# Splitting the attention's projection weights ahead of time, during the first MLP, with the parts kept in DRAM

## The chip, the cores and the metric

The kernel runs on one core of a Trainium2 chip. The metric is the device time of one execution in microseconds, as a median over runs. The engines are TensorE (PE, with its weight loads as PEld), VectorE (DVE), ScalarE (ACT), GpSimd (POOL) and SyncE (SP), which here only issues transfers.

## The reference

A decoder trunk of two layers over 528 positions (16 learned meta tokens and 512 inputs) of width 1024, all in float32. Layer 0 mixes with an mLSTM head group and a gated linear recurrence, layer 1 with differential attention; each is followed by an MLP with a squared ReLU:

```python
for layer in range(DEPTH):
    hn = _rmsnorm(h, norm_mix[layer])
    h = h + (_ab_mixer(hn, ...) if layer % 2 == 0 else _diff_attn(hn, c_w_in, ..., c_w_out, ...))
    h = h + _sq_relu_mlp(_rmsnorm(h, norm_mlp[layer]), mlp_w1[layer], mlp_w2[layer])
h = _rmsnorm(h, norm_final)

def _diff_attn(hn, w_in, ...):
    q, k, v = _split(hn @ w_in, C_SPLITS)      # 8 heads; q and k rotated on 16 of 64 dims
    ...                                        # two softmaxes per head, subtracted; norm per head
    return o @ w_out
```

## The kernel before

All large products run in float32r, at three products for one: each float32 operand is split into a high part (a cast to float32r) and a low part (the rest, a subtraction), and high x high, high x low and low x high are added up in PSUM.

**Weight units.** All projection weights lie in DRAM as 225 units `wu[u]` of 128 x 1024 floats (512 KB). Their order of use is the list `seq`: units 0 to 48 for layer 0's input projections, 49 to 64 for its output projection, 65 to 128 for the first MLP (`U_MLP0`), 129 to 152 for the attention's q, k and v (`U_QKV`, three per head), 153 to 160 for its output projection (`U_OUT1`), 161 to 224 for the second MLP (`U_MLP1`). `get_w` hands out the next unit and first calls `emit_load` until two units beyond it are on their way. `emit_load` (L148) transfers the unit into a buffer `raw` (two buffers, pool `wr`), casts it on ACT into `wh` (L159) and subtracts on DVE, or on POOL for the positions listed in `POOL_L`, into `wl` (`sub`, L115). `wh` and `wl` have three buffers each (pool `wp`), so ACT's cast of a unit waits until PE is done with the unit three places earlier. The cast and the subtraction stand under `soon()`, a raised priority. `unit_mm` (L177) multiplies a unit with eight blocks of the activations.

**MLP.** `mlp` (L651) works in four quarters: eight units of the first matrix, each followed by a squared ReLU (DVE L662, ACT L664) and the split of the result, and eight units of the second matrix, each added to the residual `h` (DVE L673).

**Attention.** `attend` (L730) runs the three units of a head. The q and k results are copied out (ACT L741), rotated with a shuffle (L747), two products (POOL L748, DVE L749) and a sum (L750), split (L754, L758) and moved into the layouts for the score products by transfers `st<-rh` and `st<-rl` (SP, L765 and L766). Between and inside the units stand the steps of earlier heads, placed by hand in `SLOTS`: `sstep` (scores L805 to L809, row maximum L811 to L816, exponential L819), `tstep` (transposes L841, their split L853), `vstep` (transposes of v, L787), `ostep` (L865) and `fstep` (norm, L875 to L881). The output projection (L903) interleaves with the last heads.

**Order.** The Tile framework orders the instructions of every engine at compile time, by priority and a model of the durations, and inserts the waits; each engine's queue then runs in that order. PSUM has four buffers for the units and four for the rest.

Of the kernel before, what the change touches and what calls it, by code (L numbers as in the profile page):

```python
# [10 lines left out]
F32 = mybir.dt.float32  # L11
F32R = mybir.dt.float32r
# [4 lines left out]
P = 128  # L17
# [20 lines left out]
U_MLP0 = 65  # L38
# [14 lines left out]

POOL_OPS = "Mm"

POOL_L = {5, 33, 43, 44, 52, 126, 140, 143, 149, 151, 155, 159, 161, 164}
N_S = 31

N_KZ = 3
LOAD1 = 9  # L60
# [4 lines left out]
C_NMIX0, C_NMIX1, C_NMLP0, C_NMLP1, C_NFIN, C_MN, C_CW, C_CB, C_BR, C_BI, C_LAM, C_SUB, C_IB, C_FB = (  # L65
    0, 8, 16, 24, 32, 40, 48, 80, 88, 96, 104, 112, 113, 114)
# [3 lines left out]
def unit_of(t):  # L70
    a = [int(c) for c in t[1:]]
    if t[0] == "q":
        return U_HEAD + 6 * a[0] + a[1]
    if t[0] == "e":
        return U_GATE
    if t[0] == "o":
        return U_O + a[0]
    return U_LRU + 4 * (a[0] // 2) + a[0] % 2 + (2 if t[0] == "g" else 0)


def trunk(tc, hT, wu, wri, pk, lv, rope, gf, out, probe=None):
    nc = tc.nc
    ctx = ExitStack()

    def dump(name, ap):
        if probe and name in probe:
            nc.sync.dma_start(out=probe[name], in_=ap)

    with ctx:
        cp = ctx.enter_context(tc.tile_pool(name="cp", bufs=1))  # L90
        wr = ctx.enter_context(tc.tile_pool(name="wr", bufs=2))
        wp = ctx.enter_context(tc.tile_pool(name="wp", bufs=3))
# [3 lines left out]
        dr = ctx.enter_context(tc.tile_pool(name="dr", bufs=1, space=bass.MemoryType.DRAM))  # L96
# [7 lines left out]
        def sc(name, dt=F32, w=T):  # L104

            return big.tile([P, T], dt, tag="s", name=name, bufs=N_S)

        def xt(name):

            hi = big.tile([P, T], F32R, tag="x", name=name + "h", bufs=32)  # L110
            lo = big.tile([P, T], F32R, tag="x", name=name + "l", bufs=32)
            return hi, lo

        def sub(eng, o, a, b):
            eng.tensor_tensor(out=o, in0=a, in1=b, op=ALU.subtract)  # L115

        def split(hl, src, sl=slice(0, T), eng=None):
            nc.scalar.copy(hl[0][:, sl], src)
            sub(eng or nc.vector, hl[1][:, sl], src, hl[0][:, sl].bitcast(F32))
# [15 lines left out]
        def soon():  # L135
            return tc.high_priority(offset=BOOST)
# [4 lines left out]

        seq = list(range(N_UNIT))
        ready = []
        seq[0:U_OUT0] = [unit_of(t) for t in PLAN if t[0] in "qeocg"]
        seq[U_OUT0:U_OUT0 + 16] = [U_OUT0 + (8 + i) % 16 for i in range(16)]
        state = {"next": 0, "use": 0}

        def emit_load():  # L148
            i = state["next"]
            u = seq[i]  # L150
            raw = wr.tile([P, 1024], F32, tag="raw", name=f"raw{i}")
            nc.sync.dma_start(out=raw, in_=wu[u])
            if u >= N_UNIT - 8:
                wh, wl = (wp.tile([P, 1024], F32R, tag="wf" + p, name=f"w{p}{i}", bufs=8) for p in "hl")
            else:
                wh = wp.tile([P, 1024], F32R, tag="wh", name=f"wh{i}")
                wl = None if u == U_GATE else wp.tile([P, 1024], F32R, tag="wl", name=f"wl{i}")
            with soon():
                nc.scalar.copy(wh, raw)  # L159
                eng = nc.gpsimd if i in POOL_L else nc.vector  # L160
                if u == U_GATE:

                    hi, r = (a.rearrange("p (k c) -> p k c", k=KB) for a in (wh, raw))
                    sub(eng, hi[:, :, 64:100], r[:, :, 0:36], hi[:, :, 0:36].bitcast(F32))
                else:
                    sub(eng, wl, raw, wh.bitcast(F32))
            ready.append((wh, wl))
            state["next"] += 1

        def get_w(u):  # L170
            while state["next"] <= min(state["use"] + 2, len(seq) - 1):
                emit_load()
            assert seq[state["use"]] == u
            state["use"] += 1
            return ready.pop(0)

        def unit_mm(u, x, lo=0, n=T, mid=None):  # L177

            wh, wl = get_w(u)
            mid = mid or state.pop("mid", None)  # L180
            cuts = [(lo, n)] if n <= 512 else [(0, HV), (HV, HV)]
            ps = [mmt(f"mm{u}") for _ in cuts]
            for k in range(KB):
                if k == KB // 2 and mid:
                    mid()
                c = slice(k * P, (k + 1) * P)
                terms = [(wh, x[k][0]), (wh, x[k][1])] + ([(wl, x[k][0])] if wl is not None else [])
                for j, (w, xx) in enumerate(terms):
                    for p, (s, m) in zip(ps, cuts):
                        nc.tensor.matmul(p[:, :m], w[:, c], xx[:, s:s + m], start=(k == 0 and j == 0),  # L190
                                         stop=(k == KB - 1 and j == len(terms) - 1))
            return [(p[:, :m], slice(s, s + m)) for p, (s, m) in zip(ps, cuts)]
# [33 lines left out]
        def norm_x(h, gc, lo, tag, late=False):  # L226

            x = [xt(f"{tag}x{k}") for k in range(KB)]
            fin = []
            for k in range(KB):  # L230
                hk = h[:, k, lo:]
                fin_x = nc.scalar.activation(out=x[k][0][:, lo:], in_=hk, func=AF.Copy, scale=pc(gc + k))  # L232
                nc.vector.scalar_tensor_tensor(out=x[k][1][:, lo:], in0=hk, scalar=pc(gc + k),
                                               in1=x[k][0][:, lo:].bitcast(F32), op0=ALU.mult, op1=ALU.subtract)
                if not late:
                    norm_sq(h, lo, k, fin)
            return (x, fin_x) if late else (x, fin)
# [9 lines left out]
        def norm_r(terms, lo, tag, le=False):  # L247

            w = (T - lo) // 2
            ps = [axt("nps") for _ in range(2)]  # L250
            for b in range(2):
                nc.tensor.matmul(ps[b][:, :w], ones, terms[0][:, lo + b * w:lo + (b + 1) * w], start=True, stop=True)
            v = sc("nv")
            for b in range(2):
                idn = nc.scalar.activation(out=v[:, lo + b * w:lo + (b + 1) * w], in_=ps[b][:, :w], func=AF.Identity,
                                     bias=epsc, scale=1.0 / 1024)
            rstd = big.tile([P, T], F32, tag="rstd", name=tag + "rstd", bufs=2)
            rsq_of(rstd[:, lo:], v[:, lo:], lambda nm: sc(nm)[:, lo:], le=le, after=idn)
            return rstd, v
# [16 lines left out]

        h0 = big.tile([P, KB, T], F32, tag="h", name="h0")
        emit_load()
        for k in range(KB):
            nc.sync.dma_start(out=h0[:, k, :], in_=hT[:, k, :])  # L280
            if k == LOAD1:
                emit_load()
# [365 lines left out]
        dump("h1", h)  # L648


        def mlp(u0, gc, lo, tag, last=None):  # L651
            n = T - lo
            mx, terms = norm_x(h, gc, lo, tag)
            for q in range(4):
                a = []
                for j in range(KB):
                    ps = unit_mm(u0 + q * 16 + j, mx, lo, n)
                    if q == j == 0:
                        rs, _ = norm_r(terms, lo, tag)
                    t = sc("rt")  # L660
                    for p, tk in ps:
                        nc.vector.scalar_tensor_tensor(out=t[:, tk], in0=p, scalar=0.0, in1=rs[:, tk],  # L662
                                                       op0=ALU.max, op1=ALU.mult)
                    nc.scalar.activation(out=t[:, lo:], in_=t[:, lo:], func=AF.Square)  # L664
                    a.append(xt(f"a{j}"))
                    split(a[j], t[:, lo:], slice(lo, T))
                if q == 3 and last:
                    last(a)
                else:
                    for c in range(KB):  # L670
                        ps = unit_mm(u0 + q * 16 + 8 + c, a, lo, n)
                        for p, tk in ps:
                            nc.vector.tensor_tensor(out=h[:, c, tk], in0=p, in1=h[:, c, tk], op=ALU.add)  # L673

        mlp(U_MLP0, C_NMLP0, 0, "m")
        dump("h2", h)


# [212 lines left out]
        for part, ks in enumerate(OUT_K):  # L891
            w = None
            for i, (c, k) in enumerate((c, k) for c in range(KB) for k in ks):
                if i % 8 == 0:
                    w = get_w(U_OUT1 + (6 if part else 0) + i // 8)
# [29 lines left out]
        def final_quarter(a):  # L925
            w = [get_w(N_UNIT - 8 + k) for k in range(KB)]
            for t in range(4):
# [23 lines left out]
                with soon():  # L951
                    if len(spans) == 3:
# [10 lines left out]
                                                   op1=ALU.mult)  # L963
                    nc.sync.dma_start(out=out[t * P:(t + 1) * P, 512:1024], in_=z2)
        mlp(U_MLP1, C_NMLP1, NM, "n", last=final_quarter)


# [93 lines left out]
```

## Time and profile before

| | |
|---|---|
| Median of three runs | 1483.99 us (1482.4 to 1485.17) |
| The profiled execution's own time | 1483.99 us |
| Its span, first to last instruction | 1481.9 us |
| Mean granted clock of TensorE | 0.996 |
| Transfers | 140.79 MB, mean 95 GB/s |
| Casts of weight units on ACT (L159) | 225, 1050 ns each |
| Subtractions of weight units on DVE, on POOL | 210, 1277 ns each; 14, 2418 ns each |

How to read it: a line such as "906.47 0.52 PE L841 MATMUL pt<-ident,e 128\*72 128x128 f32 x3 [1.51 <-DVE vr L774]" says that at 906.47 us from the start PE ran three such matmuls of line 841, which took 0.52 us together, and that it had been idle for 1.51 us, until DVE's instruction of line 774 ended. In a table by stretch the columns are: the stretch, its length, the busy time of each engine with its number of instructions, the granted clock of TensorE (1 is full speed), the mean share of time in which the 16 DMA engines were busy, and GB/s.

### The profile page before, as it was taken

What the parts mean: (1) busy time and instruction counts of PE and PEld (TensorE: products, weight loads), DVE (VectorE), ACT (ScalarE), POOL (GpSimd) and SP (SyncE); (2) the same over time, 40 slices, a digit from 0 to 9 for tenths busy, and PEclk for the clock granted to TensorE, in tenths of its full rate; (3) what the DMA queues carried; (4) which work ended last, traced back from release to release, by engine and by line L of the source; (5) the groups of instructions that cost most, each with busy time, mean ns of one, the idle gap of its engine ahead of it and who ended that gap; (6) DMA issues with size and microseconds to landing.
All of it is one profiled execution on the core that took longest, in us unless ns stands there. A gap on an engine that the chain in (4) does not pass through costs nothing.

```text
span 1481.9 us, 24188 instructions
## 1 busy us (share of the span) xinstructions
PE 1445.6 (98%) x9970; PEld 1344.5 (91%) x9970; DVE 837.7 (57%) x1489; ACT 631.9 (43%) x1090; POOL 126.7 (9%) x100
## 2 busy tenths in 40 slices
PE   8999999999999999999999999999999999999998
PEld 8999999999999999999999988888787888888886
DVE  5867745667545434344344589999865434343452
ACT  6455744647234213233143445655654223132342
POOL 4000001000011000000002211111132000000001
PEclk9999999999999999999999999999999999999999
DMA  7332323231222322322323343323122233233241
GB/s 254 96 114 79 99 72 121 72 100 48 90 93 86 92 95 86 100 86 87 100 86 92 110 115 94 94 87 100 58 86 79 92 100 94 92 100 95 91 124 47
DMA packets 48794, 140.79 MB, mean 95 GB/s; under 512 B 9226, under 2 KB 10775, under 8 KB 48684
## 3 DMA queue, kind: packets, MB, share of 16 engines
q1 hardware_dynamic: 48108, 138.21, 30.4%
q8 instruction: 78, 1.28, 0.4%
q10 hardware_dynamic: 576, 1.05, 0.2%
q14 instruction: 32, 0.26, 0.1%
HBM read 128.55 MB, written 2.16 MB: 88 GB/s over the span
## 4 chain that ended last, share of the span: by engine, by line
PE 85%; DVE 8%; ACT 3%; issue 2%; DMA 1%; POOL 0%; SPq 0%; DVEq 0%; ACTq 0%
PE mm L190 73%; PE mf L940 3%; PE mo L903 3%; PE pnum L393 1%; PE pss L375 1%; PE pg L586 1%; DVE wl L115 1%; DVE qr L750 1%; DMA st<-rh 1%; DVE kz L115 1%; PE pt L841 1%; DVE mx L814 1%; PE po L865 1%; PE psc L805 1%; DVE qs L747 1%
## 5 line engine op out<-in xcount | busy, mean ns | idle before, releaser
L159 ACT CAST wh<-raw 128x1024 fp32r<-128x1024 f32 x225 | 236.3, 1050 | 615.8 <-PE mm L190 510.1
L115 DVE TENSOR_TENSOR wl<-raw,wh 128x1024 fp32r<-128x1024 f32 x210 | 268.1, 1277 | 74.1 <-ACT wh L159 72.0
L673 DVE TENSOR_TENSOR h<-mm,h 128x264 f32<-128x264 f32 (+1 forms) x88 | 41.3, 500 | 188.6 <-PE mm L190 188.6
L243 POOL TENSOR_TENSOR nsq<-nsq 128x528 f32<-128x528 f32 (+1 forms) x28 | 48.4, 1729 | 447.6 <-DVE wl L115 336.0
L662 DVE SCALAR_TENSOR_TENSOR rt<-mm,mrstd 128x264 f32<-128x264 f32 x64 | 24.7, 428 | 89.1 <-PE mm L190 89.1
L662 DVE SCALAR_TENSOR_TENSOR rt<-mm,nrstd 128x512 f32<-128x512 f32 x32 | 22.1, 692 | 79.7 <-PE mm L190 79.6
L115 POOL TENSOR_TENSOR wl<-raw,wh 128x1024 fp32r<-128x1024 f32 x14 | 33.9, 2418 | 230.3 <-ACT wh L159 148.2
L819 ACT ACTIVATE e<-psc,nb 128x264 f32<-128x264 f32 (+3 forms) x80 | 38.1, 481 | 21.3 <-DVE nb L816 18.5
L664 ACT ACTIVATE rt<-rt 128x528 f32<-128x528 f32 (+1 forms) x64 | 40.6, 636 | 2.8 <-DVE rt L662 2.8
L748 POOL TENSOR_TENSOR qr<-qr,tb 128x512 f32<-128x512 f32 (+1 forms) x16 | 26.5, 1654 | 144.9 <-DVE nb L816 82.1
L811 DVE TENSOR_REDUCE mx<-psc 128x1 f32<-128x264 f32 (+3 forms) x80 | 33.2, 429 | 5.8 <-PE psc L809 5.7
L949 POOL TENSOR_TENSOR zg<-z,gfr 128x512 f32<-128x512 f32 x4 | 5.2, 1296 | 343.6 <-issue 326.9
L633 DVE TENSOR_TENSOR h<-mm,h 128x264 f32<-128x264 f32 x32 | 12.4, 428 | 38.7 <-PE mm L190 38.7
L805 PE MATMUL psc<-st,st 128*128 128x264 f32 (+3 forms) x80 | 26.6, 333 | 7.2 <-DVE v1l L115 3.6
L805 PEld LDWEIGHTS psc<-st,st 128*128 128x128 f32 x80 | 15.3, 192 | 14.9 <-ACT e L819 5.3
L853 ACT CAST pp<-pt 128x128 fp32r<-128x128 f32 (+2 forms) x64 | 20.8, 343 | 18.5 <-DVE pp L115 14.0
L190 PE MATMUL mm<-ax0h,wh 128*128 128x264 f32 x98 | 22.0, 297 | 6.1 <-ACT ax0h L232 6.1
L115 DVE TENSOR_TENSOR pp<-pt,pp 128x256 fp32r<-128x256 f32 (+2 forms) x64 | 23.7, 378 | 1.3 <-ACT pp L853 1.1
L806 PE MATMUL psc<-kz,st 128*128 128x264 f32 (+3 forms) x80 | 24.0, 300 | 0.0
L841 PE MATMUL pt<-ident,e 128*72 128x128 f32 (+1 forms) x112 | 18.3, 278 | 5.7 <-ACT e L819 4.2
L190 PE MATMUL mm<-a4h,wl 128*128 128x264 f32 (+1 forms) x88 | 22.6, 316 | 0.0
L190 PE MATMUL mm<-a1h,wh 128*128 128x264 f32 (+1 forms) x88 | 22.5, 316 | 0.0
(802 smaller groups left out, 4772.9 us busy)
## 6 DMA issues: line engine op xcount, KB each, us to landing
raw<-wu SPq DMA_DIRECT2D x225, 512.0 KB
h<-hT SPq DMA_DIRECT2D x16, 264.0 KB
st<-rh SPq DMA_DIRECT2D x32, 132.0 KB
st<-rh SPq DMA_DIRECT2D x16, 128.0 KB
st<-rl SPq DMA_DIRECT2D x16, 128.0 KB
cb<-crow SPq DMA_DIRECT2D x4, 264.0 KB
erb<-crow SPq DMA_DIRECT2D x4, 264.0 KB
rawg<-wri SPq DMA_DIRECT2D x4, 256.0 KB
```

The costliest lines, as they stand in the source:

```text
L115: eng.tensor_tensor(out=o, in0=a, in1=b, op=ALU.subtract)
L159: nc.scalar.copy(wh, raw)
L190: nc.tensor.matmul(p[:, :m], w[:, c], xx[:, s:s + m], start=(k == 0 and j == 0), stop=(k == KB - 1 and j == len(terms) - 1))
L243: nc.gpsimd.tensor_tensor(out=fin[0][:, lo:], in0=fin[0][:, lo:], in1=sq[:, lo:], op=ALU.add)
L662: nc.vector.scalar_tensor_tensor(out=t[:, tk], in0=p, scalar=0.0, in1=rs[:, tk], op0=ALU.max, op1=ALU.mult)
L664: nc.scalar.activation(out=t[:, lo:], in_=t[:, lo:], func=AF.Square)
L673: nc.vector.tensor_tensor(out=h[:, c, tk], in0=p, in1=h[:, c, tk], op=ALU.add)
L805: nc.tensor.matmul(d[:, :m], qS[c][:, qs], kS[c][:, s0:s0 + m], start=True, stop=False)
L811: nc.vector.tensor_reduce(out=mx[:, 2 * c + r:2 * c + r + 1], in_=d[:, :m], axis=AX.X, op=ALU.max)
L819: nc.scalar.activation(out=e[:, s0:s0 + m], in_=d[:, :m], func=AF.Exp, bias=nb, scale=0.125, accum_out=ss[:, c + 2 * r:c + 2 * r + 1])
L903: nc.tensor.matmul(ps, w[ww][:, b], co[k][xx][:, NM:], start=(k == ks[0] and j == 0), stop=(k == ks[-1] and j == 2))
L940: nc.tensor.matmul(pss[n][:, :m], a[k][aa][:, tk], w[k][ww][:, f0:f0 + m], start=(k == 0 and i == 0), stop=(k == KB - 1 and i == 2))
```

## The change

For the positions 129 to 160 of `seq` (`AHEAD`: the 24 units of the attention's q, k and v and the eight of its output projection) the split is made during the first MLP. After every second unit of that MLP `make_ahead` is called, 32 times, and once more after it. A call writes the two parts of the unit made by the call before to DRAM (`parts`, two tiles of 512 KB for each unit), then loads the next unit through the same two `raw` buffers, casts it on ACT and subtracts on DVE into the tiles `wah` and `wal` (one buffer each), without raised priority. When such a unit's turn comes, `emit_load` transfers both parts from DRAM straight into `wh` and `wl`; there is no cast and no subtraction then. Six of these positions leave `POOL_L`.

```diff
-POOL_L = {5, 33, 43, 44, 52, 126, 140, 143, 149, 151, 155, 159, 161, 164}
+POOL_L = {5, 33, 43, 44, 52, 126, 161, 164}
+AHEAD = range(129, 161)
...
+        parts = [[dr.tile([P, 1024], F32, name=f"part{i}{p}") for p in "hl"] for i in AHEAD]
...
         def emit_load():
             i = state["next"]
             u = seq[i]
+            if i in AHEAD:
+                wh, wl = (wp.tile([P, 1024], F32R, tag="w" + p, name=f"w{p}{i}") for p in "hl")
+                for w, part in zip((wh, wl), parts[i - AHEAD[0]]):
+                    nc.sync.dma_start(out=w.bitcast(F32), in_=part)
+                ready.append((wh, wl))
+                state["next"] += 1
+                return
             raw = wr.tile([P, 1024], F32, tag="raw", name=f"raw{i}")
...
+        ahead = list(AHEAD)
+        made = []
+
+        def make_ahead():
+
+            while made:
+                i, hl = made.pop(0)
+                for w, part in zip(hl, parts[i - AHEAD[0]]):
+                    nc.sync.dma_start(out=part, in_=w.bitcast(F32))
+            if ahead:
+                i = ahead.pop(0)
+                raw = wr.tile([P, 1024], F32, tag="raw", name=f"rawa{i}")
+                nc.sync.dma_start(out=raw, in_=wu[seq[i]])
+                hl = [wp.tile([P, 1024], F32R, tag="wa" + p, name=f"wa{p}{i}", bufs=1) for p in "hl"]
+                nc.scalar.copy(hl[0], raw)
+                sub(nc.vector, hl[1], raw, hl[0].bitcast(F32))
+                made.append((i, hl))
...
-        def mlp(u0, gc, lo, tag, last=None):
+        def mlp(u0, gc, lo, tag, last=None, between=None):
...
                     split(a[j], t[:, lo:], slice(lo, T))
+                    if between and j % 2:
+                        between()
...
                             nc.vector.tensor_tensor(out=h[:, c, tk], in0=p, in1=h[:, c, tk], op=ALU.add)
+                        if between and c % 2:
+                            between()
 
-        mlp(U_MLP0, C_NMLP0, 0, "m")
+        mlp(U_MLP0, C_NMLP0, 0, "m", between=make_ahead)
+        make_ahead()
```

## The prediction, made before the changed kernel ran

> **What bounds the kernel now.** I read the page's busy times first, then a table of busy time by stretch (columns: stretch, its length, busy us with instruction counts of PE, PEld, DVE, ACT and POOL, granted clock, DMA share, GB/s).
>
> ```profile
> span 1481.9 us, 24188 instructions
> PE 1445.6 (98%) x9970; PEld 1344.5 (91%) x9970; DVE 837.7 (57%) x1489; ACT 631.9 (43%) x1090; POOL 126.7 (9%) x100
> 460.00:830.00 370.00, 370.00 (x3048) 369.45 (x3047) 156.45 (x233) 116.73 (x148) 13.18 (x7) 1.00 0.30 92
> 835.00:865.00 30.00, 28.16 (x201) 26.28 (x200) 22.48 (x42) 12.36 (x23) 5.27 (x3) 1.00 0.39 106
> 865.00:1068.00 203.00, 187.80 (x1249) 167.74 (x1249) 188.92 (x477) 116.91 (x321) 33.12 (x18) 0.99 0.32 92
> ```
>
> TensorE bounds the whole, but the stages differ. In the first MLP (460 to 830) PE is busy for all 370 us while DVE has 213 us free and ACT 253. In seven heads' worth of attention (865 to 1068) PE stands idle for 203 - 187.80 = 15.20 us, and VectorE is busy for 93% of the time. Only what shortens those 15 us, or the 30 - 28.16 = 1.84 us of the passage before them, can make the kernel faster; the 370 us of the first MLP can only be lost.
>
> Which wait ends the idle times? PE's own order of time, with the idle time ahead in brackets, and the same for POOL and DVE:
>
> ```profile
> 906.47 0.52 PE L841 MATMUL pt<-ident,e 128*72 128x128 f32 x3 [1.51 <-DVE vr L774]
> 935.65 0.52 PE L841 MATMUL pt<-ident,e 128*72 128x128 f32 x3 [1.75 <-ACT e L819]
> 957.48 0.36 PE L805 MATMUL psc<-st,st 128*128 128x264 f32 x1 [0.66 <-DVE v1l L115]
> 975.31 0.73 PE L865 MATMUL po<-pp,v1h 72*128 72x512 f32 x2 [0.31 <-ACT e L819]
> 993.44 0.52 PE L841 MATMUL pt<-ident,e 128*72 128x128 f32 x3 [1.59 <-ACT e L819]
> 1014.37 1.12 PE L875 MATMUL poq<-osq,ones 128*128 128x512 f32 x2 [1.80 <-ACT osq L870]
> 1053.20 0.33 PE L805 MATMUL psc<-st,st 128*128 128x144 f32 x1 [1.87 <-ACT e L819]
> 903.28 2.39 POOL L115 TENSOR_TENSOR wl<-raw,wh 128x1024 fp32r<-128x1024 f32 x1 [8.31 <-ACT wh L159]
> 932.21 2.37 POOL L115 TENSOR_TENSOR wl<-raw,wh 128x1024 fp32r<-128x1024 f32 x1 [9.42 <-ACT wh L159]
> 989.99 2.38 POOL L115 TENSOR_TENSOR wl<-raw,wh 128x1024 fp32r<-128x1024 f32 x1 [9.48 <-ACT wh L159]
> 1009.81 2.45 POOL L115 TENSOR_TENSOR wl<-raw,wh 128x1024 fp32r<-128x1024 f32 x1
> 1049.75 2.38 POOL L115 TENSOR_TENSOR wl<-raw,wh 128x1024 fp32r<-128x1024 f32 x1 [9.48 <-ACT wh L159]
> 929.56 0.15 DVE L814 TENSOR_TENSOR mx<-mx 128x1 f32<-128x1 f32 x1
> 932.64 1.96 DVE L814 TENSOR_TENSOR mx<-mx 128x1 f32<-128x1 f32 x1
> 1009.93 2.90 DVE L750 TENSOR_TENSOR qr<-qr,qs 128x528 f32<-128x528 f32 x1
> 1012.92 0.63 ACT L754 CAST rh<-qr 128x528 fp32r<-128x528 f32 x1 [4.85 <-DVE qr L750]
> ```
>
> POOL splits five weight units here, and each time one of the five long idle times of PE follows 3 to 5 us later. The link is VectorE: the one-column maximum of L814 takes 0.15 us at 929.56 and 1.96 us at 932.64, beside POOL's split of 932.21; at 1009.93 the rotation's sum is held until POOL's split ends. The exponential or the copy behind it comes late, and PE waits. The five gaps sum to 1.51 + 1.75 + 1.59 + 1.80 + 1.87 = 8.52 us of the 15.20. Between 950 and 978 us no POOL split falls, and the two gaps of those 28 us are 0.66 and 0.31.
>
> **The change part by part.** The sum is made against the profiled execution, 1483.99 us (span 1481.9, and 2.1 around it), which is also the median of the three runs.
>
> *Splits taken out of the attention.* The same table for the instructions on wl (DVE) and wh (ACT) alone:
>
> ```profile
> 865.00:1068.00 203.00, 26.21 (x16) 0.99 0.32 92
> 865.00:1068.00 203.00, 21.15 (x21) 0.99 0.32 92
> ```
>
> POOL's five splits go, so five gaps go: -8.5 us. (The sixth unit that left POOL's list is split after 1068; I cost it at nothing.) VectorE loses 26.21 of 188.92 us, ACT 21.15 of 116.91. The other idle times there, 15.20 - 8.52 = 6.7 us, end on DVE and ACT work that queues behind the splits. Bounds: all of it (-6.7), or none, as the POOL-free stretch keeps about 1 us in 28 with VectorE still splitting. I take half: -3.3.
>
> *The clock.* After the gap of 1.87 us:
>
> ```profile
> 1052.00:1056.00 4.00, 2.80 (x11) 2.46 (x12) 3.41 (x16) 2.67 (x11) 0.13 (x1) 0.73 0.47 135
> 1056.00:1060.00 4.00, 4.00 (x21) 3.53 (x21) 3.40 (x11) 1.41 (x5) 0.00 (x0) 0.84 0.00 0
> ```
>
> The granted clock is 0.73 and 0.84 over 4 us each, so (0.27 + 0.16) x 4 = 1.7 us of TensorE work is lost on top of the gap. With the gap gone: -1.7. The Trainium skill (TensorE: Matmul & The Clock Gate, section "HAM oscillation — how this bites in real kernels") lets the clock fall only after idle gaps of more than about 3.4 us; by that rule this term would be zero and the forecast 1473.2. This trace differs, with its 0.73 right after 1.87 us of idleness, and the measurement decides.
>
> *The passage into the attention.* On the chain of waits one split stands between the rotations:
>
> ```profile
> 842.48 2.23 DVE wl L115
> ```
>
> It goes. PE's idle time there is 1.84 us in all, so the gain is between 0 and 1.8; I take half, -0.9.
>
> *The extra work of the first MLP.* Rows from it, and the kernel's first load:
>
> ```profile
> 463.39 36.03 SPq L152 DMA_DIRECT2D raw<-wu  x7
> 474.62 1.23 DVE L115 TENSOR_TENSOR wl<-raw,wh 128x1024 fp32r<-128x1024 f32 x1 [0.19 <-ACT wh L159]
> 479.34 1.05 ACT L159 CAST wh<-raw 128x1024 fp32r<-128x1024 f32 x1 [3.54 <-PE mm L190]
> 485.15 1.05 ACT L159 CAST wh<-raw 128x1024 fp32r<-128x1024 f32 x1 [3.54 <-PE mm L190]
> 0.73 0.39 SPq L152 DMA_DIRECT2D raw<-wu  x1
> 4.39 1.04 ACT L159 CAST wh<-raw 128x1024 fp32r<-128x1024 f32 x1 [2.38 <-DMA raw<-wu]
> raw<-wu SPq DMA_DIRECT2D x225, 512.0 KB
> 0.00:37.00 37.00, 30.39 (x223) 29.95 (x224) 21.29 (x35) 24.09 (x38) 16.40 (x20) 1.00 0.73 254
> ```
>
> A unit takes 485.15 - 479.34 = 5.8 us, two units 11.6. Per two units the change adds a copy (1.05) to ACT, a subtraction (1.23) to DVE, one load and two writes of 512 KB. In all, 32 x 1.23 = 39 us go into DVE's 213 free us, 32 x 1.05 = 34 into ACT's 253; ACT idles 3.54 us in each unit. POOL's share of DVE's time is small there (13.18 us in 370). Transfers rise from two to five per 11.6 us: 92 x 2.5 = 230 GB/s, share 0.30 x 2.5 = 0.75, which the kernel's start reached (254 at 0.73). SP issues 128 transfers more in all, some 0.39 us each, 50 us of a queue that now issues one per 5.8 us.
>
> The waits matter more. The new loads share the two raw buffers: 23.2 us of buffer time per two units. A load holds one for 4.39 - 0.73 = 3.7 us, then 1.05 + 1.23: 6.0 us. Three make 18; the two writes take 0.30 x 5.8 = 1.74 us of the DMA engines each, so if they stand ahead of one load, 18 + 3.5 = 21.5. It fits, by 1.7 us. ACT's copy of an advance unit also waits for the previous write (one buffer for each part); behind it in ACT's queue stand the next unit's copy and the squares, and DVE's subtraction waits for it. The cover is the unit's lead: a weight is copied when a slot comes free, two units before its use, 11.6 - 1.05 - 1.23 = 9.3 us. Term: 0.
>
> *Reading the parts back.* A load now waits on SP for the PE unit that frees its slots, not for a raw buffer. Behind it in SP's queue stand the rotated halves (`st`), but those depend on a later product of PE than the load does. PE has two whole units (11.6 us) plus attention before the use; two transfers need 3.7 + 1.74 = 5.4 us. Term: 0 for the weights; what it does to `st` is a rival.
>
> *A new order.* The planner orders the whole attention anew. No row shows what comes of it. Bounds: no new wait, or one in each of the five places (+8.5); a gain is excluded, since all the idle time there is is counted above. The nearest rows are the POOL-free stretch's: 0.66 + 0.31 = 0.97 us, 6.8 in seven heads, where my terms so far leave 3.4. I add one gap of the largest size, +1.9, and end between the two.
>
> Sum: -8.5 - 3.3 - 1.7 - 0.9 + 1.9 = -12.5; 1484.0 - 12.5 = **1471.5 us**. Own range: from 1465.3 (all idle time gone: 8.5 + 6.7 + 1.7 + 1.8 = 18.7) to 1479 (half of the POOL gaps stay).
>
> **The rivals.**
>
> *The raw buffers run short in the first MLP (slower).* If the three loads and their queueing need more than 23.2 us per two units, PE falls behind by half the excess each time, and from 23.2 + 2 x 9.3 / 32 = 23.8 on the lead is used up. With both writes ahead of each load: 18 + 3 x 3.5 = 28.5, or 2.65 x 32 - 9.3 = 75 us lost. Halfway between 21.5 and 28.5 it is 25.0: 0.9 x 32 - 9.3 = 19.5, **1491 us**. For it: only 1.7 us spare, and the advance copies are not given the raised priority of the others. Against: the loads of the unit in use are traced ahead of the writes, and PE's 370 of 370 us shows how much the lead covers today. The Trainium skill (DMA: Bandwidth & Descriptors, section "Latency and other measured facts") puts an HBM access at 0.2 us on average and 2 us at high load; 1.8 us more on each of three loads would give 26.9 and, estimated so, 50 us lost, near 1522. No run here shows such a latency.
>
> *The read-back delays the rotated halves (no change).* On the chain of waits:
>
> ```profile
> 853.05 3.33 DMA st<-rh
> 974.37 3.29 DMA st<-rh
> 1034.11 3.32 DMA st<-rh
> ```
>
> These transfers are waited for three times. If a read of both parts stands ahead of them each time, each is 2 x 1.74 = 3.5 us later: +10.4, **1482 us**. For it: twice the weight bytes on the same queue. Against: reads start at a unit's end, and a rotation takes some microseconds more before `st` is ready.
>
> *The gain is half (the locks stay).* POOL still runs the rotation's product of L748, which can hold VectorE too, and another late step takes each gap's place: half of 12.5, **1478 us**.
>
> **How the numbers follow.** Forecast 0.60, short buffers 0.20, delayed halves 0.10, half gain 0.10. 0.2% is 3 us, about what a measurement tells from no change. Faster: 0.60 + 0.08 = 0.68; within: 0.11; slower: 0.21, nearly all from the buffers. The range runs from 1465 to 1495, which takes in the middle of the slower case and leaves out its far half.
>
> **What would show it.** Right: no POOL split from 865 to 1068, no one-column DVE instruction near 1.9 us, PE idle under 8 us in the seven heads, DVE near 163 us there, PE still at 370 of 370 in the first MLP at a DMA share near 0.75. Wrong: PE gaps in the first MLP ended by ACT's or DVE's split (short buffers); score products ended by the `st` transfers (delayed halves); gaps of 1.5 us or more in new places (order).

## The result, and the profile after

The change makes the kernel slower: 1502.65 us (1502.13 to 1503.27) against 1484.16 us before, a ratio of 1.0123 (95% interval 1.0107 to 1.0139). The forecast of 1471.5 us and its range up to 1495 do not hold it. The attention gains some 15 us, a little more than was forecast; the first MLP loses more than twice as much.

The same place of the program in both traces, the transposes of a head's v (`vstep`) from the first head to the last: first the two rows of before, then the two of after.

```profile
866.29 0.75 PE L787 MATMUL pv<-ident,vr 128*72 128x128 f32 x5
1065.20 0.71 PE L787 MATMUL pv<-ident,vr 128*72 128x128 f32 x5
...
896.63 0.71 PE L820 MATMUL pv<-ident,vr 128*72 128x128 f32 x5
1082.32 0.71 PE L820 MATMUL pv<-ident,vr 128*72 128x128 f32 x5
```

The first head comes 896.63 - 866.29 = 30.3 us later. From there the seven heads take 185.7 us where they took 198.9: 13.2 us won. The span grows by 1500.3 - 1481.9 = 18.4 us, so 30.3 lost, 13.2 won, and 1.3 lost behind the heads. Busy time by stretch, columns as before (stretch, length, busy us and count of PE, PEld, DVE, ACT, POOL, clock, DMA share, GB/s); the first row is of before, the other two of after, with the first MLP last:

```profile
866.30:1065.20 198.90, 184.02 (x1228) 164.83 (x1227) 185.50 (x470) 113.46 (x311) 33.12 (x18) 0.99 0.32 91
...
896.60:1082.30 185.70, 179.13 (x1221) 162.10 (x1220) 154.56 (x453) 93.93 (x288) 20.93 (x13) 1.00 0.50 153
460.00:865.00 405.00, 381.44 (x3045) 377.12 (x3044) 189.87 (x263) 145.87 (x177) 13.81 (x8) 0.97 0.66 210
```

In the heads PE's idle time falls from 14.9 to 6.6 us and VectorE's load from 185.5 to 154.6. The passage from the attention's first unit (the product of its last block, `dx7h`) to the first head, before and after:

```profile
833.30:866.30 33.00, 30.84 (x215) 28.46 (x214) 23.77 (x44) 14.64 (x27) 5.27 (x3) 1.00 0.39 104
866.90:896.60 29.70, 29.60 (x213) 28.07 (x212) 17.72 (x41) 10.37 (x25) 5.27 (x3) 1.00 0.66 213
```

It takes 3.3 us less. So the first MLP itself lost 30.3 + 3.3 = 33.6 us, and the attention gained 3.3 + 13.2 - 1.3 = 15.2 in all.

In the first MLP, where PE had no idle time, it now stands idle for 23.6 us, and the mean granted clock is 0.97. Where it waits, from PE's order of time in the changed kernel, and what ACT does ahead of the last of these gaps:

```profile
611.33 0.81 PE L218 MATMUL mm<-a7h,wh 128*128 128x264 f32 x2 [5.23 <-ACT a7h L120]
713.96 0.81 PE L218 MATMUL mm<-a7h,wh 128*128 128x264 f32 x2 [5.26 <-ACT a7h L120]
817.59 0.81 PE L218 MATMUL mm<-a7h,wh 128*128 128x264 f32 x2 [5.37 <-ACT a7h L120]
...
815.28 1.04 ACT L169 CAST wh<-raw 128x1024 fp32r<-128x1024 f32 x1 [4.61 <-DMA raw<-wu]
816.23 0.64 ACT L692 ACTIVATE rt<-rt 128x528 f32<-128x528 f32 x1
816.90 0.63 ACT L120 CAST a7h<-rt 128x528 fp32r<-128x528 f32 x1
```

The name in the bracket is not the cause. PE waits for the last activation of a quarter, `a7h`; ACT makes it late because the weight's cast ahead of it in ACT's queue waits 4.61 us for a load. The same product in the kernel before, at the first and the last of these three places:

```profile
600.48 0.41 PE L190 MATMUL mm<-a7h,wh 128*128 128x264 f32 x2
...
786.62 0.41 PE L190 MATMUL mm<-a7h,wh 128*128 128x264 f32 x2
```

From the first place to the last are two quarters, 16 turns of two units each. They take 206.3 us where they took 186.1: 12.9 us a turn in place of 11.6. Behind such a gap the clock is low for some microseconds:

```profile
816.00:820.00 4.00, 2.41 (x9) 2.17 (x10) 2.52 (x4) 2.33 (x4) 0.00 (x0) 0.50 0.67 210
820.00:824.00 4.00, 4.00 (x25) 4.00 (x24) 3.14 (x4) 2.44 (x4) 0.00 (x0) 0.66 0.36 145
```

Why is the load late? The chain of waits of the changed kernel within one turn of two units, and SP's queue in the next:

```profile
636.95 3.55 DMA rawa<-wu
...
640.57 1.06 ACT wah L194
...
642.07 5.47 DMA raw<-wu
...
647.62 1.06 ACT wh L169
...
648.70 0.60 DVE wl L117
...
649.96 3.41 DMA rawa<-wu
```

```profile
649.96 0.33 SPq L192 DMA_DIRECT2D rawa<-wu  x1
654.54 0.33 SPq L188 DMA_DIRECT2D part144h<-wah  x1
654.97 1.21 SPq L162 DMA_DIRECT2D raw<-wu  x2
656.23 0.50 SPq L188 DMA_DIRECT2D part144l<-wal  x1
662.70 0.33 SPq L192 DMA_DIRECT2D rawa<-wu  x1
```

The loads take turns. SP issues the advance load; the next instruction in its queue, the write of that unit's high part, waits until ACT has cast it (654.54); only behind it stand the two unit loads, with the write's bytes ahead of them (in the turn before, the first of the two landed in 5.5 us); the next advance load waits for the buffer that the first of them frees. One turn takes 662.70 - 649.96 = 12.74 us, and PE needs 11.6. That is 1.1 us in each of 32 turns, 36 us, against the first MLP's 33.6: of the lead of 9.3 us only some 3 were of use.

### The profile page after: what moved, and what is told of

It reads as the page before. It is cut to its first block, busy times and chain, and to the rows that moved or that the text cites. A ratio compares the mean times of both kernels' runs of the same rounds, so it can differ in the third digit from the quotient of the medians.

```text
span 1500.3 us, 24426 instructions
## 1 busy us (share of the span) xinstructions
PE 1451.0 (97%) x9970; PEld 1349.1 (90%) x9970; DVE 829.2 (55%) x1495; ACT 633.5 (42%) x1090; POOL 113.1 (8%) x94
## 4 chain that ended last, share of the span: by engine, by line
PE 66%; DMA 15%; DVE 8%; ACT 6%; issue 3%; POOL 1%; SPq 1%; ACTq 0%; POOLq 0%; DVEq 0%
PE mm L218 56%; DMA raw<-wu 8%; DMA rawa<-wu 6%; PE mf L973 3%; DVE wl L117 2%; PE mo L936 2%; ACT wh L169 2%; ACT wah L194 2%; PE pnum L421 1%; POOL qr L781 1%; DMA st<-rh 1%; PE pss L403 1%; PE pg L614 1%; DVE kz L117 1%; DVE qr L783 1%
## 5 line engine op out<-in xcount | busy, mean ns | idle before, releaser
L169 ACT CAST wh<-raw 128x1024 fp32r<-128x1024 f32 x193 | 202.5, 1050 | 534.8 <-PE mm L218 313.1
L117 DVE TENSOR_TENSOR wl<-raw,wh 128x1024 fp32r<-128x1024 f32 x184 | 227.1, 1235 | 163.1 <-ACT wh L169 162.6
L117 DVE TENSOR_TENSOR wal<-rawa,wah 128x1024 fp32r<-128x1024 f32 x32 | 40.2, 1257 | 65.4 <-ACT wah L194 61.4
L194 ACT CAST wah<-rawa 128x1024 fp32r<-128x1024 f32 x32 | 33.6, 1050 | 74.2 <-DMA rawa<-wu 72.9
L218 PE MATMUL mm<-a7h,wh 128*128 128x264 f32 (+1 forms) x88 | 23.9, 332 | 17.6 <-ACT a7h L120 17.6
L117 POOL TENSOR_TENSOR wl<-raw,wh 128x1024 fp32r<-128x1024 f32 x8 | 19.2, 2396 | 204.9 <-ACT wh L169 204.9
L218 PEld LDWEIGHTS mm<-a7h,wh 128*128 128x128 f32 x88 | 15.0, 197 | 19.5 <-ACT a7h L120 18.4
L218 PE MATMUL mm<-a6h,wh 128*128 128x264 f32 (+1 forms) x88 | 22.9, 319 | 4.3 <-ACT a6h L120 4.3
L117 DVE TENSOR_TENSOR pp<-pt,pp 128x128 fp32r<-128x128 f32 (+2 forms) x64 | 23.7, 381 | 3.2 <-ACT pp L886 2.1
```

The costliest lines, as they stand in the source:

```text
L194: nc.scalar.copy(hl[0], raw)
```

## The experiments

Three explanations stood against each other: SP's order (a write that waits, ahead of the loads), the two raw buffers with a sum of times too large for them, and the traffic (DMA share 0.66 in place of 0.30).

**The writes behind the loads.** Nothing but the place of the writes in SP's queue is changed:

```diff
-            nc.sync.dma_start(out=raw, in_=wu[u])
+            state["load"] = nc.sync.dma_start(out=raw, in_=wu[u])
...
-                    nc.sync.dma_start(out=part, in_=w.bitcast(F32))
+                    with tc.issue_after(state["load"].ins):
+                        nc.sync.dma_start(out=part, in_=w.bitcast(F32))
```

> The writes of the parts stay on SP's queue but stand behind the raw loads that were traced ahead of them. Queue order (the first part's write waits for ACT's cast of the advance unit and holds up the next loads behind it on SP): two units of the first MLP take 11.6 us again instead of 12.75, PE's idle time there is under 5 us, and the time is 1471 us, between 1467 and 1478. Two raw buffers too few, or too much traffic: same transfers and same buffers, so 1495 to 1503 us.

Measured: 1469.03 us, ratio to before 0.9902 (0.9885 to 0.9919). The first MLP by stretch, SP's queue, and the chain of waits over the same 28 us:

```profile
460.00:830.00 370.00, 370.00 (x3042) 369.28 (x3041) 194.64 (x263) 146.79 (x177) 12.33 (x8) 1.00 0.69 228
```

```profile
643.35 0.33 SPq L193 DMA_DIRECT2D rawa<-wu  x1
649.02 2.60 SPq L162 DMA_DIRECT2D raw<-wu  x2
651.68 0.43 SPq L189 DMA_DIRECT2D part145h<-wah  x1
652.15 1.51 SPq L189 DMA_DIRECT2D part145l<-wal  x1
654.94 0.33 SPq L193 DMA_DIRECT2D rawa<-wu  x1
```

```profile
639.99 28.07 PE mm L219 x232
```

PE is busy for 370 of 370 us at a DMA share of 0.69 and 228 GB/s, with the same transfers, the same two buffers, and the same order of casts on ACT. A turn is 11.6 us and the chain is PE alone. So neither the traffic nor the sum of the buffer times made the loss: one place in SP's queue did, worth 1502.65 - 1469.03 = 34 us.

**The writes on ACT's queue.**

```diff
-                    nc.sync.dma_start(out=part, in_=w.bitcast(F32))
+                    nc.scalar.dma_start(out=part, in_=w.bitcast(F32))
```

> The writes of the parts are issued from ACT's queue. Queue order: nothing on SP waits for the cast any more, so 1471 us, between 1467 and 1480 (ACT itself waits up to 1.3 us for each subtraction). Traffic or buffers: the same bytes and buffers, 1495 to 1503 us.

Measured: 1507.18 us, ratio 1.0159 (1.014 to 1.0178): a miss, slower than the changed kernel, though no load waits behind a write any more. SP's queue and ACT's in one turn:

```profile
653.36 0.33 SPq L192 DMA_DIRECT2D rawa<-wu  x1
659.28 1.47 SPq L162 DMA_DIRECT2D raw<-wu  x2
666.48 0.33 SPq L192 DMA_DIRECT2D rawa<-wu  x1
...
651.02 1.05 ACT L169 CAST wh<-raw 128x1024 fp32r<-128x1024 f32 x1 [5.29 <-DMA raw<-wu]
656.95 1.05 ACT L194 CAST wah<-rawa 128x1024 fp32r<-128x1024 f32 x1 [4.88 <-DMA rawa<-wu]
657.90 1.04 ACT L169 CAST wh<-raw 128x1024 fp32r<-128x1024 f32 x1
```

With the writes on ACT the planner put the advance cast between the casts of the two units. The second unit's load has long landed but keeps its raw buffer until ACT has cast the advance unit; the other buffer serves everything else, one after another: 13.1 us a turn. The theory had to be widened: what costs is that the loads of a turn wait for each other, through SP's order or through ACT's order and the shared buffers.

**No write waits, and no write beside the loads.** The first MLP's advance loads, casts and subtractions stay, the writes take a constant tile, and the attention is as before:

```diff
-                    nc.sync.dma_start(out=part, in_=w.bitcast(F32))
+                    nc.sync.dma_start(out=part, in_=fixed)
...
-            if i in AHEAD:
+            if False:
```

> The first MLP as in the changed kernel (advance load, cast, subtraction, 64 writes of 512 KB), but the writes take a constant tile, so they never wait for the cast; the attention is as in the kernel before and the written parts are not used. Queue order: the first MLP is at its old length, 1484 to 1488 us. Traffic: the same bytes beside the loads cost the same 30 us as in the changed kernel, with no gain in the attention: 1510 to 1516 us.

Measured: 1493.66 us, ratio 1.0065 (1.0049 to 1.0081), between the two expectations and in neither. It is no test of the traffic in the first MLP: writes that wait for nothing were placed much earlier, in layer 0 (339 GB/s between 100 and 150 us), and the first MLP ran at 133 GB/s. The larger part of the loss lies ahead of it: its first product runs at 461.47 us in place of 455.24, 6.2 us later than in the kernel before. From there to the attention's first unit only 5.1 us more are lost. What the run shows is the chain without writes, with ACT's casts in the order of the run before:

```profile
642.74 0.33 SPq L194 DMA_DIRECT2D rawa<-wu  x1
648.73 1.47 SPq L162 DMA_DIRECT2D raw<-wu  x2
654.71 0.33 SPq L194 DMA_DIRECT2D rawa<-wu  x1
```

A turn takes 12.0 us even then, 0.4 over PE's. That is 13 us in 32 turns; 5.1 of them reach PE, and the rest is less than the lead.

**The reading half alone.**

```diff
-                for w, part in zip((wh, wl), parts[i - AHEAD[0]]):
+                for w, part in zip((wh, wl), parts[0]):
...
-        ahead = list(AHEAD)
+        ahead = [AHEAD[0]]
```

> Only the reading half: one unit is split ahead and every position of the attention reads that one pair of parts (so the projections are computed with one unit's weights; 31 advance loads, casts, subtractions and 62 writes are left out). If the loss lies in the first MLP alone and the attention gains what the trace shows: 1484 - 13 = 1471 us, between 1468 and 1474. If reading the parts delayed the rotated halves, 1480 or more.

Measured: 1469.36 us, ratio 0.9903 (0.9886 to 0.992). Every projection of the attention uses one unit's weights here, with as many transfers and products in the attention as in the changed kernel. Without the work in the first MLP the change gains 14.6 us, the same as with that work and the writes behind the loads. No delay by the reads shows.

**The first MLP's half alone**, queues as in the changed kernel, the attention and POOL's list as in the kernel before:

```diff
-            if i in AHEAD:
+            if False:
```

> The first MLP's queues as in the changed kernel (on SP: advance load, write of the high part, two unit loads, write of the low part; on ACT the same order of casts), the attention as in the kernel before; the written parts are not used. If the whole loss arises in the first MLP from that order: two units take 12.75 us there again, 1484 + 30 = 1514 us, between 1508 and 1518. If the loss needed the attention's reads: near 1484.

Measured: 1517.78 us, ratio 1.0239 (1.0222 to 1.0256), 34.7 us lost. SP's queue shows the same turn, 12.74 us:

```profile
648.79 0.33 SPq L192 DMA_DIRECT2D rawa<-wu  x1
653.40 0.33 SPq L188 DMA_DIRECT2D part144h<-wah  x1
...
661.53 0.33 SPq L192 DMA_DIRECT2D rawa<-wu  x1
```

**A raw buffer of its own for the advance loads**, with the writes on SP and then on ACT:

```diff
-                raw = wr.tile([P, 1024], F32, tag="raw", name=f"rawa{i}")
-                nc.sync.dma_start(out=raw, in_=wu[seq[i]])
+                raw = wr.tile([P, 1024], F32, tag="rawa", name=f"rawa{i}", bufs=1)
+                with tc.issue_after(state["load"].ins):
+                    nc.sync.dma_start(out=raw, in_=wu[seq[i]])
```

> The advance loads get a raw buffer of their own; the writes stay on SP and are placed by the planner, in part ahead of unit loads. Serial chain (advance load, cast, write, unit load, cast, subtraction, next advance load, each waiting for the one before through the shared buffers and SP's order): the chain is cut at the shared buffer, a turn is under 11.6 us, 1470 us, between 1466 and 1476. If a write that waits ahead of unit loads costs the same whatever the buffers: 1495 to 1503.

> Writes issued from ACT's queue and an own raw buffer for the advance loads. Serial chain through the shared buffer (which gave 13.1 us for two units with the writes on ACT): cut, 1470 us, between 1466 and 1478. If ACT's waiting for the subtraction ahead of each low part's write was what cost 23 us with the writes on ACT: still 1495 to 1507.

Measured: 1469.45 us (0.9906, 0.9891 to 0.9921) and 1468.07 us (0.9899, 0.9885 to 0.9914). The first MLP of the two, by stretch:

```profile
460.00:830.00 370.00, 370.00 (x3057) 369.87 (x3055) 192.53 (x260) 143.57 (x175) 13.60 (x8) 1.00 0.67 229
...
460.00:830.00 370.00, 370.00 (x3045) 369.23 (x3044) 191.95 (x262) 144.84 (x176) 12.88 (x8) 1.00 0.67 230
```

The edits do more than give a buffer: `issue_after` also ties the advance load to the unit load traced ahead of it. In the first run that changed the order on SP. The high part's write now stands behind one of the two unit loads (load at 658.21 us, write at 658.78, next load at 664.02), so this run is no test of a write right ahead of both. In the second, the loads stand on SP in the same order as in the run with the writes on ACT, one advance load and two unit loads; with a buffer of its own for the former a turn is 11.6 us in place of 13.1, and ACT's waiting at the writes costs nothing. So the order and the shared buffers made the loss together: with the buffers still shared, a better order on SP was enough, and with the writes on ACT, a buffer more.

**Writes of 16 columns.**

```diff
-                    nc.sync.dma_start(out=part, in_=w.bitcast(F32))
+                    nc.sync.dma_start(out=part[:, :16], in_=w[:, :16].bitcast(F32))
```

> As the run with the first MLP's part alone, with the same order on SP, but each write takes 16 of 1024 columns (the parts are not complete and not used; the attention is as in the kernel before). Serial chain whose links are lengthened by the writes' bytes: without them a unit load lands in 3.6 us instead of 5.2, a turn of the chain takes 11.0 to 11.9 us against PE's 11.6, so 1484 to 1494 us. If the waiting alone makes the loss, bytes or not: 1510 us or more.

Measured: 1491.48 us, ratio 1.0059 (1.0039 to 1.008). Its chain of waits over one turn:

```profile
540.18 3.41 DMA rawa<-wu
...
543.68 1.06 ACT wah L194
...
544.77 1.24 DVE wal L117
...
546.02 3.59 DMA raw<-wu
...
549.71 1.06 ACT wh L169
...
550.79 1.24 DVE wl L117
...
552.04 3.40 DMA rawa<-wu
```

552.04 - 540.18 = 11.86 us: two loads of 3.4 to 3.6, two casts, two subtractions, one after the other. Without bytes ahead of it a unit load lands 1.9 us sooner than the 5.47 of the changed kernel, and most of the loss is gone. (Most turns of this run take 11.7 to 12.0 us, a few up to 12.7.) The write still waits for the cast here, ahead of two unit loads, so the wait alone costs little; the larger part came with the write's bytes. One caution: the order on ACT differs by one place from the changed kernel's, so the wait and the bytes are not quite separated.

**Only POOL's six positions taken away from the kernel before.**

```diff
-POOL_L = {5, 33, 43, 44, 52, 126, 140, 143, 149, 151, 155, 159, 161, 164}
+POOL_L = {5, 33, 43, 44, 52, 126, 161, 164}
```

> The kernel before, with only the six positions taken off POOL's list, so that VectorE makes all subtractions of the attention. Hold-ups by POOL's splits: the five gaps of 8.5 us and the lost clock of 1.7 us go, and VectorE gets 5 x 1.23 = 6 us more in seven heads: 1476 us, between 1473 and 1480. VectorE's load as such is the limit: 1484 to 1490 us.

Measured: 1476.00 us, ratio 0.995 (0.9935 to 0.9965). The seven heads by stretch:

```profile
865.00:1068.00 203.00, 195.02 (x1293) 173.71 (x1294) 190.70 (x498) 123.10 (x335) 21.64 (x13) 1.00 0.32 92
```

PE's idle time is 203 - 195.02 = 8.0 us where it was 15.2, while VectorE is busier than before, 190.70. The longest of VectorE's one-column maxima (L814) in this stretch takes 0.16 us; in the kernel before it took 2.02. Half of the attention's gain, 7 of some 15 us, is a list of six numbers.

## Why the prediction was wrong, point by point

*The step that failed* is the first MLP's term of 0; 33.6 us were lost there. It added up the time for which three loads hold two buffers (21.5 of 23.2 us) as if both buffers always worked side by side. They did not: in the changed kernel and in every slow variant the loads came one after another, 12.7 us a turn, 13.1 with the writes on ACT, 12.0 without writes. The durations in that sum were right (3.7 us for a load assumed, 3.4 to 3.6 measured). What was missing was SP's queue: the step named what stands behind the new cast on ACT and behind the subtraction on DVE, but not that the write waits on SP for the cast and then goes, with its 512 KB, ahead of the next two unit loads. With the writes behind these loads the term was 0 indeed. How much of the loss is the wait and how much the bytes stays partly open; the run with 16 columns puts the larger part on the bytes.

*The rival of the short buffers* had the place and the sign and was given 0.20. Its price of 1491 us was a halfway value of a sum that was the wrong sum, and its argument against itself, that the unit loads are traced ahead of the writes, was no argument: the planner put the write ahead of them. The Trainium skill's 2 us for an HBM access under load (DMA: Bandwidth & Descriptors, section "Latency and other measured facts") is not seen: at a DMA share of 0.66 an advance load still landed in 3.4 us.

*The lead of 9.3 us* was counted as cover for everything, but it covers the weights only. PE's long waits are for an activation (`a7h`) in the middle of each quarter, whose cast stands behind the late weight's cast in ACT's queue. This is the second thing that the step left out.

*The attention* came out near the forecast: 12.5 us expected in all, 15.2 in the changed kernel, 14.6 for the reading half alone. Its terms were less right than their sum, which is in part luck. POOL's splits with the clock were put at 10.2; taking them away alone gave 7.1, with the five splits added to VectorE's work. The passage was put at 0.9, at most 1.8, and gave 3.3.

*The delayed halves* (1482 us) and *the half gain* (1478 us) are both refuted by the reading half alone, at 1469.36 us.

*DMA share*: 0.75 forecast for the first MLP, 0.66 to 0.69 measured; not the limit.

## What to carry to other kernels

When a store is added to the queue that also issues loads, ask first what the store waits for and which loads stand behind it; here one place in that queue was worth 34 us and turned a gain of 1% into a loss. A budget of buffer time says whether a schedule is possible, not whether in-order queues will run it: write down the chain load, cast, store, load and compare one turn of it with the unit's time. Where planner and queues are hard to foresee, a buffer that is not shared cuts the chain.

## What the runs showed of the hardware that was not expected

VectorE busy for 190.70 of 203 us, 94%, left PE only 8 us idle: its load as such was not the limit there, and taking five splits off POOL was worth 7 us although VectorE then had more to do. And mixed writes and loads at 228 to 230 GB/s cost PE nothing in the three runs in which it was busy for 370 of 370 us. What counted was which transfer stood ahead: in the changed kernel a 512 KB load landed in 3.4 to 3.6 us with nothing just ahead of it, and in 5.5 us behind a write of the same size.
